# Gate stage with stationary tokens, three of eight pairs of k-tiles by seven block products, weight units of 1 MB, and part of h kept in DRAM

## The chip, the cores and the metric

The kernel runs on one core of one Trainium2 chip. The metric is the time of one execution on the device in microseconds (us), and the kernel before stands at the median of three runs. The engines are named as the profile names them: PE multiplies matrices (PEld is its loading of stationary operands), DVE, ACT and POOL work on vectors, SP issues most transfers.

## The reference

One layer of an encoder works on 256 tokens of width 2048, in float32: half a feed-forward step, a mixer (a long convolution beside differential attention), and a second half feed-forward step, each followed by a layer norm. The change is in the two feed-forward steps, whose inner width is 5632:

```python
def swiglu(x, w_gate, w_up, w_down):
    return (jax.nn.silu(x @ w_gate) * (x @ w_up)) @ w_down

x = layer_norm(ALPHA * x + 0.5 * swiglu(x, ffn1_w_gate[i], ffn1_w_up[i], ffn1_w_down[i]), ln1_g[i], ln1_b[i])
...
x = layer_norm(ALPHA * x + 0.5 * swiglu(x, ffn2_w_gate[i], ffn2_w_up[i], ffn2_w_down[i]), ln3_g[i], ln3_b[i])
```

The hidden rows are h = silu(x @ w_gate) * (x @ w_up), 256 x 5632.

## The kernel before, in words

**Precision.** Every float32 operand is cut into a high part (a cast on ACT) and a low part (a subtraction on DVE), and a product is the sum of three matmuls: high by high, high by low and low by high. `mm3` issues the three.

**Weights.** All weights pass once from DRAM, in pieces of 512 KB that the list `units` holds in the order of use. `fetch` issues their transfers on SP's queue into four raw slots, `prepare` cuts the next two pieces ahead of use (ACT at L176, DVE at L177) and `nextunit` hands the next piece to PE. `tick`, called once for each piece, moves the side work on (`beside`, `once`): generators that load vectors, compute the convolution's filter or finish an earlier block.

**Gate stage.** 22 blocks of 256 hidden columns. In `ws_block` the weights are stationary (128 x 128) and the tokens move: for each of the 16 k-tiles and each 128 columns, one matmul of 512 columns (the weights' high part by the tokens' high and low parts side by side, L395) and one of 256 (the low part by the tokens' high part, L396). A block's result lies transposed in PSUM, 256 tokens along the row. `gate` adds its two halves (`ws_sum`), applies silu, multiplies (POOL) and cuts h, which stays in SBUF as `hh` and `hl` for the whole down stage.

**Down stage.** Four chunks of 512 output columns. The h tiles are stationary, the weights move, 512 columns in each matmul (L94 to L96); a piece of 512 KB is two k-tiles, which is 12 matmuls. `scale_residual` loads and scales the rows of the residual `res`, and `last_vectors` the vectors of the last layer norm.

**Order of work.** Each engine runs its own instructions in order. A scheduler places them from the dependencies; `after` adds an order by hand, and the pools' buffer counts set what waits for what. The first feed-forward step has the tag 1, the last one 2 or 3. FFN1 and FFN2 below are those two steps.

Of the kernel before, what the change touches and what calls it, by code (L numbers as in the profile page):

```python
# [11 lines left out]
F32 = mybir.dt.float32  # L12
# [24 lines left out]
RAW = 4  # L37
READY = 2
AHEAD = 5
# [35 lines left out]
def kernel(ctx: ExitStack, tc: tile.TileContext, a: dict, out: bass.AP):  # L75
# [3 lines left out]
    wp = ctx.enter_context(tc.tile_pool(name="wp", bufs=4))  # L79
# [32 lines left out]

    units = []

    def ws_units(tag, w, c0, ws=None):

        for kq in range(KD // 4):
            for m, v in enumerate(ws or [w]):
                units.append((v[0][kq * 512:(kq + 1) * 512, c0:c0 + 256].rearrange("(k p) c -> p k c", p=P), 4, 256, f"{tag}_{kq}_{m}"))

    def as_units(tag, w, c0, kt):

        for ku in range(kt // 2):
            units.append((w[0][ku * 256:(ku + 1) * 256, c0:c0 + 512].rearrange("(k p) c -> p k c", p=P), 2, 512, f"{tag}_{ku}"))

    def ffn_units(tag, wg, wu, wd):
        for fb in range(FF // 256):
            ws_units(f"{tag}g{fb}", None, fb * 256, [wg, wu])
        for c in range(4):
            as_units(f"{tag}d{c}", wd, c * 512, KF)  # L130
# [8 lines left out]
    for k in range(KD):  # L139
        units.append((a["w_out"][0][k * P:(k + 1) * P, :1024].rearrange("p (k c) -> p k c", k=2), 2, 512, f"wo_{k}"))  # L140
# [4 lines left out]
    st = {"dma": 0, "split": 0, "use": 0}  # L145
    raws, parts = {}, {}
    hold = {}

    def halves(i, k):

        n = (4, 2)[i] if i < 2 else 1
        return [slice(q * k // n, (q + 1) * k // n) for q in range(n)]

    def fetch(n):
        while st["dma"] < min(n, len(units)):
            i = st["dma"]
            src, k, c, name = units[i]
            raws[i] = wp.tile([P, k, c], F32, tag="raw", name=f"raw{name}", bufs=RAW)
            for s_ in halves(i, k):
                nc.sync.dma_start(out=raws[i][:, s_], in_=src[:, s_])  # L160
            st["dma"] += 1

    def prepare(n):
        while st["split"] < min(n, len(units)):
            i = st["split"]
            _, k, c, name = units[i]
            late = i - (len(units) - LEAD)
            if 0 <= late < 4:

                hi, lo = (xx[:, 4 * late + 2 * q:4 * late + 2 * q + 2].rearrange("p k a l -> p k (a l)") for q in range(2))  # L170
            else:
                hi = wp.tile([P, k, c], F32R, tag="whi", name=f"hi{name}")
                lo = wp.tile([P, k, c], F32R, tag="wlo", name=f"lo{name}")
            raw = raws.pop(i)
            for s_ in halves(i, k):
                i1 = nc.scalar.copy(out=hi[:, s_], in_=raw[:, s_])  # L176
                i2 = nc.vector.tensor_tensor(out=lo[:, s_], in0=raw[:, s_], in1=hi[:, s_].bitcast(F32), op=ALU.subtract)  # L177
                if hold:
                    after(i1, hold["act"])
                    after(i2, hold["dve"])  # L180
                if i == 0 and s_.stop == 2:
                    xt_first(1, i1, i2)
            parts[i] = (hi, lo)
            st["split"] += 1
# [24 lines left out]
    def nextunit():  # L209
        i = st["use"]  # L210
        st["use"] += 1
        fetch(i + 1 + AHEAD)
        prepare(i + 1 + READY)
        tick()
        return parts.pop(i)
# [18 lines left out]
    for kp in range(KD // 2):  # L234
# [6 lines left out]
        if kp in (0, 1, 3):  # L241
            fetch({0: 1, 1: 2, 3: 4}[kp])
# [36 lines left out]

    def xt_first(kp, a1=None, a2=None):  # L280
# [12 lines left out]
    def xt_chunk(tag, c, g, b):  # L293
        for kp in (2 * c, 2 * c + 1):
# [17 lines left out]
            if kp == 1:  # L312
                hold["act"], hold["dve"] = i1, i2

# [120 lines left out]
    def ffn(tag, first, down_side=None, gate_side=None, filler=None, lead=2, between=None):  # L435
        with tc.tile_pool(name=f"ffn{tag}", bufs=1, reuse_waits="tile") as fp:
            hh = fp.tile([P, KF, L], F32R, name=f"hh{tag}")
            hl = fp.tile([P, KF, L], F32R, name=f"hl{tag}")

            def gate(f, pg, pu):  # L440
                sg = sm.tile([P, L], F32, tag="sg", name=f"sg{tag}_{f}")
                ws_sum(sg, pg)
                nc.scalar.activation(out=sg, in_=sg, func=AF.Silu)
                hf = sm.tile([P, L], F32, tag="hf", name=f"hf{tag}_{f}")
                ws_sum(hf, pu)
                nc.gpsimd.tensor_tensor(out=hf, in0=hf, in1=sg, op=ALU.mult)  # L446
                split(hh[:, f, :], hl[:, f, :], hf, nc.gpsimd)

            first(0)
            for fb in range(FF // 256):  # L450
                if fb == 12 and gate_side is not None:
                    beside(gate_side)
                ps = [[bank(f"ps{tag}_{fb}_{m}_{t}") for t in range(2)] for m in range(2)]
                for kq in range(4):
                    for m in range(2):
# [688 lines left out]
```

## Time and profile before

| what | value |
|---|---|
| median of 3 runs | 1941.37 us (1941.0 to 1942.09) |
| profiled execution | 1940.2 us, its span 1938.4 us |
| PE busy | 1921.0 us (99%) |
| DVE busy | 1214.8 us (63%) |
| ACT busy | 926.5 us (48%) |
| POOL busy | 298.3 us (15%) |
| granted TensorE clock, mean | 0.998 |
| read from DRAM | 366.28 MB |

The span runs from the first instruction to the last; the profiled execution's own time is 1.8 us longer. Busy shares are averages over the whole span: an engine at 63% can still be late in one place. PE's busy time is the sum of modelled ends, so its pace is read from the starts of its matmuls.

### The profile page before, as it was taken

Reading aid. Unit: us, or ns where it says so; the run is one execution under the profiler, and the core shown is the slowest. Engines: PE = TensorE matmul, PEld = TensorE weight load, DVE = VectorE, ACT = ScalarE, POOL = GpSimd, SP = SyncE. Lnnn points to the kernel's source line nnn. Section 1 sums busy time; section 2 is a strip of 40 time slices with the busy share of each in tenths; the row PEclk is TensorE's granted clock in tenths of the full one; section 3 lists DMA queues with packets and bytes.
Section 4 is the critical chain, followed back from the end, with each engine's and each line's share of the span. In section 5 each row is a group of like instructions: output and inputs, shape, how many; then the busy total and the mean of one; then the engine's idle time right before and its main releaser. Section 6 shows DMA issues by size and latency. Waiting matters only on the chain. (4 is left out here: it accounts for less than half of the span.)

```text
span 1938.4 us, 27298 instructions
## 1 busy us (share of the span) xinstructions
PE 1921.0 (99%) x10360; PEld 1650.8 (85%) x10360; DVE 1214.8 (63%) x1555; ACT 926.5 (48%) x1336; POOL 298.3 (15%) x327
## 2 busy tenths in 40 slices
PE   9999999999999999999999999999999999999999
PEld 7888888888888888888888888888888888888887
DVE  6555556555566656899978766755555555544555
ACT  5454444455444445555555544545444445433332
POOL 4221111112100001112222011311211112100000
PEclk9999999999999999999999999999999999999999
DMA  8665656665666656755575445856566665565553
GB/s 286 211 192 185 195 188 199 186 193 186 206 207 226 211 193 204 236 176 163 176 218 164 161 155 162 278 188 192 188 192 189 190 190 185 193 195 192 193 193 131
DMA packets 295028, 376.47 MB, mean 194 GB/s; under 512 B 13331, under 2 KB 222892, under 8 KB 294896
## 3 DMA queue, kind: packets, MB, share of 16 engines
q1 hardware_dynamic: 289728, 361.38, 58.0%
q0 software_dynamic: 4736, 12.82, 2.2%
q8 instruction: 81, 1.33, 0.3%
q10 hardware_dynamic: 432, 0.52, 0.1%
q14 instruction: 51, 0.42, 0.1%
HBM read 366.28 MB, written 8.39 MB: 193 GB/s over the span
## 5 line engine op out<-in xcount | busy, mean ns | idle before, releaser
L395 PE MATMUL ps<-xx,hi1g 128*128 128x512 f32 x1408 | 489.3, 392 | 1.7 <-DVE xx L99 1.3
L395 PE MATMUL ps<-xx,hi2g 128*128 128x512 f32 x1408 | 488.7, 394 | 1.1 <-DVE xx L99 1.1
L396 PE MATMUL ps<-xx,lo1g 128*128 128x256 f32 x1408 | 393.6, 280 | 1.0 <-DVE lo1g L177 1.0
L396 PE MATMUL ps<-xx,lo2g 128*128 128x256 f32 x1408 | 390.0, 277 | 0.0
L177 DVE TENSOR_TENSOR lo2g<-raw2g,hi2g 128x1024 fp32r<-128x1024 f32 x176 | 235.0, 1337 | 178.4 <-ACT hi2g L176 178.4
L177 DVE TENSOR_TENSOR lo1g<-raw1g,hi1g 128x1024 fp32r<-128x1024 f32 (+1 forms) x180 | 230.8, 1285 | 178.6 <-ACT hi1g L176 178.3
L395 PEld LDWEIGHTS ps<-xx,hi2g 128*128 128x128 f32 x1408 | 263.9, 188 | 62.4 <-ACT xt L305 1.3
L395 PEld LDWEIGHTS ps<-xx,hi1g 128*128 128x128 f32 x1408 | 263.2, 187 | 61.0 <-ACT hi1g L176 2.3
L176 ACT CAST hi2g<-raw2g 128x1024 fp32r<-128x1024 f32 x176 | 185.2, 1053 | 187.1 <-PE ps L395 176.3
L176 ACT CAST hi1g<-raw1g 128x1024 fp32r<-128x1024 f32 (+1 forms) x180 | 185.7, 1035 | 175.2 <-PE ps L395 165.9
L396 PEld LDWEIGHTS ps<-xx,lo1g 128*128 128x128 f32 x1408 | 265.8, 189 | 2.1 <-DVE lo1g L177 1.9
L396 PEld LDWEIGHTS ps<-xx,lo2g 128*128 128x128 f32 x1408 | 264.2, 188 | 0.1
L446 POOL TENSOR_TENSOR hf<-hf,sg 128x256 f32<-128x256 f32 x88 | 66.1, 770 | 738.8 <-DVE hf L400 738.7
L177 DVE TENSOR_TENSOR lo2d<-raw2d,hi2d 128x1024 fp32r<-128x1024 f32 x84 | 103.5, 1233 | 109.2 <-ACT hi2d L176 109.0
L176 ACT CAST hi1d<-raw1d 128x1024 fp32r<-128x1024 f32 x88 | 92.7, 1053 | 125.0 <-PE pd L96 114.8
L176 ACT CAST hi2d<-raw2d 128x1024 fp32r<-128x1024 f32 x84 | 88.6, 1055 | 130.1 <-PE pd L96 123.9
L177 DVE TENSOR_TENSOR lo1d<-raw1d,hi1d 128x1024 fp32r<-128x1024 f32 x88 | 107.1, 1222 | 67.4 <-ACT hi1d L176 67.4
L395 PE MATMUL ph<-xx,hihy 128*128 128x512 f32 x384 | 137.9, 402 | 2.2 <-DVE xx L99 1.1
L95 PE MATMUL pd<-lo1d,hh 128*128 128x512 f32 (+1 forms) x356 | 137.8, 387 | 0.0
L94 PE MATMUL pd<-hi1d,hh 128*128 128x512 f32 (+1 forms) x356 | 137.8, 387 | 0.0
L96 PE MATMUL pd<-hi1d,hl 128*128 128x512 f32 (+1 forms) x356 | 137.7, 387 | 0.0
L94 PE MATMUL pd<-hi2d,hh 128*128 128x512 f32 (+1 forms) x344 | 132.1, 384 | 0.0
(387 smaller groups left out, 3090.1 us busy)
## 6 DMA issues: line engine op xcount, KB each, us to landing
raw1d<-in_ffn_w_down_dram SPq DMA_DIRECT2D x88, 512.0 KB, 4.3
raw2g<-in_ffn_w_gate_dram SPq DMA_DIRECT2D x88, 512.0 KB, 3.4
raw2g<-in_ffn_w_up_dram SPq DMA_DIRECT2D x88, 512.0 KB, 3.4
raw2d<-in_ffn_w_down_dram SPq DMA_DIRECT2D x88, 512.0 KB, 4.3
raw1g<-in_ffn_w_gate_dram SPq DMA_DIRECT2D x87, 512.0 KB, 3.5
raw1g<-in_ffn_w_up_dram SPq DMA_DIRECT2D x87, 512.0 KB, 3.8
rawhy<-in_w_in_dram SPq DMA_DIRECT2D x48, 512.0 KB, 4.3
rawat<-in_w_in_dram SPq DMA_DIRECT2D x48, 512.0 KB, 4.2
```

The source lines that it names most:

```text
L94: mm(out=o, lhsT=lh, rhs=rh, start=start, stop=False)
L95: mm(out=o, lhsT=lh, rhs=rl, start=False, stop=False)
L96: mm(out=o, lhsT=ll, rhs=rh, start=False, stop=stop)
L176: i1 = nc.scalar.copy(out=hi[:, s_], in_=raw[:, s_])
L177: i2 = nc.vector.tensor_tensor(out=lo[:, s_], in0=raw[:, s_], in1=hi[:, s_].bitcast(F32), op=ALU.subtract)
L395: mm(out=ps[t], lhsT=h[:, k, ts_], rhs=xx[:, kk].rearrange("p a l -> p (a l)"), start=kk == 0, stop=False)
L396: mm(out=ps[t][:, :L], lhsT=lo[:, k, ts_], rhs=xx[:, kk, 0, :], start=False, stop=kk == KD - 1)
L446: nc.gpsimd.tensor_tensor(out=hf, in0=hf, in1=sg, op=ALU.mult)
```

## The change

The gate stage is turned round and its loop is rebuilt:

- **Tokens are stationary and weights move**, as in the down stage. There are 11 blocks of 512 hidden columns. A product of one k-tile of tokens for one half of the tokens with 512 columns of one matrix is three matmuls of 512 columns (`mm3`). A pair of k-tiles needs eight such products (two k-tiles, two halves of the tokens, w_up and w_gate).
- **Seven instead of eight.** In the blocks after the first, three of the eight pairs (`NS = 3`) go by a seven-product scheme of the Strassen kind for 2 x 2 blocks. Its sums of tokens are made once for each feed-forward step (`sums_of`); its sums of weights, t1 to t4, are made anew for each such pair on DVE (L245 to L247), with a high part on ACT (L248) and a low part on DVE (L250). The block's results are put together on DVE (L621 to L625, and `finish`).
- **Units of 1 MB.** One unit holds both matrices of a pair of k-tiles. Kind S is a pair of seven products, kind N one of eight, and H two pieces of 512 KB as before. There are two raw slots and two slots of high and low parts, and in the gate stage a third of each (`res[:, 0]` as the raw one; `res[:, 1]` holds t1 to t4).
- **Turning h.** The block's rows of h now lie with the tokens on the partitions. `turn` makes h-transposed by four transposes on PE for each 256 columns (L556). For the first 26 of the 44 k-tiles of h the result is copied by ACT (L561) and written to DRAM from ACT's queue (L562); the last 18 (`NR = 18`) are cut and stay in SBUF (`h2`).
- **Reading h back.** In the down stage `back` reads the 26 tiles on SP's queue, 128 KB each (L659), through four small tiles, and cuts them into `h1`. Each chunk of the down stage begins with the 18 tiles that stayed.
- **Moved.** `res` being in use, the rows of the residual are loaded in the down stage (in FFN2 from a copy that POOL's queue has written to DRAM, `xn2`), `filter_net` goes from FFN1's gate stage to its down stage, and `last_vectors` goes behind `scale_residual`.

The core of the diff:

```diff
-RAW = 4
-READY = 2
-AHEAD = 5
+NS = 3
+NR = 18
+NP = KD // 2
+NF = FF // 512
...
+    def gate_order(fb):
+        if fb == 0:
+            return [(kp, False) for kp in range(NP)]
+        return [(0, True), (3, False), (1, True), (4, False), (2, True), (5, False), (6, False), (7, False)]
...
+                th, tl = (gate[q][:, st["t"] % 2] for q in ("th", "tl"))
+                st["t"] += 1
+                t = res[:, 1, :].rearrange("p (k c) -> p k c", c=512)
+                nc.scalar.copy(out=hi[:, 1:4], in_=raw[:, 1:4])
+                nc.vector.tensor_tensor(out=t[:, 0:2], in0=raw[:, 0:1].to_broadcast([P, 2, 512]), in1=raw[:, 1:3], op=ALU.subtract)
+                nc.vector.tensor_tensor(out=t[:, 2], in0=raw[:, 1], in1=t[:, 1], op=ALU.subtract)
+                nc.vector.tensor_tensor(out=t[:, 3], in0=raw[:, 3], in1=t[:, 2], op=ALU.subtract)
+                nc.scalar.copy(out=th, in_=t)
+                sub(nc.vector, lo[:, 1:4], raw[:, 1:4], hi[:, 1:4])
+                sub(nc.vector, tl, t, th)
...
-                        ws_block(ps[m], *nextunit(), kq, (lambda: first(kq + 1)) if more else None)
...
+            def turn(fb, rows, q):
+                pt = bank(f"pt{tag}_{fb}_{q}")
+                for f in range(2):
+                    for j in range(2):
+                        c = (2 * q + f) * P
+                        nc.tensor.transpose(out=pt[:, f * L + j * P:f * L + (j + 1) * P], in_=rows[j][:, c:c + P], identity=ident)
+                pv = pt.rearrange("p (f l) -> p f l", l=L)
+                k = fb * 4 + 2 * q
+                if k < n1:
+                    t = t512(f"turn{tag}_{k}")
+                    nc.scalar.copy(out=t, in_=pv)
+                    nc.scalar.dma_start(out=h1d[:, k:k + 2, :], in_=t)
+                else:
+                    k -= n1
+                    split(h2[:, 0, k:k + 2, :], h2[:, 1, k:k + 2, :], pv)
...
+                def finish(j, i):
+                    ps = pc["abcd"[2 * j + i]]
+                    if n_seven:
+                        o = (rows, up)[i][j]
+                        nc.vector.tensor_tensor(out=o, in0=ps, in1=o, op=ALU.add)
+                        ps = o
+                    if i == 0:
+                        nc.scalar.activation(out=rows[j], in_=ps, func=AF.Silu)
+                    else:
+                        nc.vector.tensor_tensor(out=rows[j], in0=ps, in1=rows[j], op=ALU.mult)
...
+                    if seven:
+                        t3, t1, t2, t4 = ((th[:, q], tl[:, q]) for q in range(4))
+                        s_last = all(not s_ for _, s_ in order[n + 1:])
+                        todo = {
+                            "1": (x_of(k1, 0), g1, s_last), "a": (x_of(k2, 0), g2, False),
+                            "b": (sum_of(kp, 2), u2, False), "7": (sum_of(kp, 3), t3, s_last),
+                            "5": (sum_of(kp, 0), t1, s_last), "6": (sum_of(kp, 1), t2, s_last),
+                            "c": (x_of(k2, 1), t4, False),
+                        }
+                        for key in ("1756abc" if n == 0 else "1ab756c"):
+                            add(key, *todo[key])
+                        turn_next()
+                        tick()
+                        if s_last:
+                            nc.scalar.copy(out=rows[0], in_=pp["1"])
+                            nc.vector.tensor_tensor(out=up[0], in0=pp["6"], in1=rows[0], op=ALU.add)
+                            nc.vector.tensor_tensor(out=rows[1], in0=pp["7"], in1=up[0], op=ALU.add)
+                            nc.vector.tensor_tensor(out=up[0], in0=pp["5"], in1=up[0], op=ALU.add)
+                            nc.vector.tensor_tensor(out=up[1], in0=pp["5"], in1=rows[1], op=ALU.add)
+                        continue
+                    for i, w in enumerate(((g1, g2), (u1, u2))):
+                        for ks in ([(0,), (1,)] if fb == 0 and not last_ else [(0, 1)]):
+                            for j in range(2):
+                                for k in ks:
+                                    add("abcd"[2 * j + i], x_of((k1, k2)[k], j), w[k], last_ and k == 1)
+                                if last_:
+                                    finish(j, i)
...
+                        if i == 0:
+                            turn_next()
+                            tick()
...
+            def back():
+                turn_next()
+                yield 1
+                turn_next()
+                yield 1
+                for k in range(n1):
+                    t = sm.tile([P, L], F32, tag="sg" if k % 2 == 0 else "hf", name=f"back{tag}_{k}")
+                    nc.sync.dma_start(out=t, in_=h1d[:, k, :])
+                    split(h1[:, 0, k, :], h1[:, 1, k, :], t)
+                    if k % 3 == 2:
+                        yield 1
```

**Where instructions stand, ACT.** The piece is the start of the seventh block of FFN1, of what ACT does before the turns of the sixth block. In the names, `hi_ring` and `hi_125` are the slots of high parts, `th` the high parts of t1 to t4, `row` the block's hidden rows, `pt` the bank of a turn. First the kernel before, at a block's end:

```order
L399 COPY sg_4_782<-ps_2_0_0_566 128x256 [waits PE_49]
L176 CAST hi1g_1_0_778<-raw1g_1_0_702 128x1024 [waits DMAHW0_49,DVE_49,PE_49]
L443 ACTIVATE sg_4_782<-sg_4_782 128x256 [waits DVE_49]
L399 COPY sg_5_792<-ps_2_0_1_567 128x256 [waits PE_49]
L399 COPY hf_4_786<-ps_2_1_0_568 128x256 [waits PE_49,Pool_49]
L443 ACTIVATE sg_5_792<-sg_5_792 128x256 [waits DVE_49]
L399 COPY hf_5_796<-ps_2_1_1_569 128x256 [waits PE_49,Pool_49]
L176 CAST hi1g_1_1_820<-raw1g_1_1_726 128x1024 [waits DMAHW1_49,Activation_49]
```

There the copies of 256 columns out of PSUM stand between casts of 1024. After the change:

```order
L198 CAST hi_ring<-raw_ring 128x2048 [waits DMAHW1_49,DMAHW2_49,PE_49,Activation_49]
L599 ACTIVATE row_5_0_1556<-row_5_0_1556 128x512 [waits DVE_49]
L599 ACTIVATE row_5_1_1557<-row_5_1_1557 128x512 [waits DVE_49]
L243 CAST hi_ring<-raw_ring 128x1536 [waits DMAHW3_49,DMAHW4_49,PE_49,Activation_49]
L198 CAST hi_125<-res 128x2048 [waits DMAHW5_49,DMAHW6_49,PE_49,Activation_49]
L248 CAST th_123<-res 128x2048 [waits DVE_49]
L561 COPY turn_20_1873<-pt_5_0_1868 128x512 [waits PE_49]
L562 DMA h1d_118<-turn_20_1873 128x512 [waits Activation_49]
L561 COPY turn_22_1897<-pt_5_1_1892 128x512 [waits PE_49]
```

The copy of `pt_5_0` now stands behind one cast of 1536 columns and two of 2048, the last of which waits for DVE's t1 to t4.

**PE.** The same place on PE: the second turn of the sixth block inside the second unit of the seventh. `pb`, `pd` and `pt` are banks of PSUM. Before, at the change from one pair of banks to the next:

```order
L396 MATMUL ps_9_0_0_1976<-xx,lo1g_1_0_1983 128x256
L395 MATMUL ps_9_0_1_1977<-xx,hi1g_1_0_1982 128x512
L396 MATMUL ps_9_0_1_1977<-xx,lo1g_1_0_1983 128x256
L395 MATMUL ps_9_1_0_1978<-xx,hi1g_1_1_2024 128x512 [waits Activation_49]
L396 MATMUL ps_9_1_0_1978<-xx,lo1g_1_1_2025 128x256 [waits DVE_49]
```

There a bank is taken over from ACT at L395, between pairs of 512 and 256 columns. After the change:

```order
L95 MATMUL pb_6_1860<-hi_ring,xx 128x512
L96 MATMUL pb_6_1860<-lo_ring,xx 128x512
L556 MATMUL pt_5_1_1892<-ident,row_5_0_1556 128x128 [waits Activation_49]
L556 MATMUL pt_5_1_1892<-ident,row_5_1_1557 128x128
L556 MATMUL pt_5_1_1892<-ident,row_5_0_1556 128x128
L556 MATMUL pt_5_1_1892<-ident,row_5_1_1557 128x128
L97 MATMUL pb_6_1860<-hi_ring,xx 128x512
L95 MATMUL pb_6_1860<-hi_ring,xx 128x512
L96 MATMUL pb_6_1860<-lo_ring,xx 128x512
L97 MATMUL pb_6_1860<-hi_ring,xx 128x512
L95 MATMUL pd_6_1906<-hi_ring,xx 128x512 [waits Activation_49]
```

The four transposes into `pt_5_1` wait for ACT, and behind them on PE's queue the first product into `pd_6` waits for ACT again.

**SP.** The start of FFN1's down stage on SP's queue: transfers of down weights, and those of h. Before:

```order
L160 DMA raw1d_0_4521<-in_ffn_w_down_dram 128x2x512 [waits DMAHW6_49,DVE_49]
L160 DMA raw1d_1_4543<-in_ffn_w_down_dram 128x2x512 [waits DMAHW7_49,DVE_49]
L160 DMA raw1d_2_4565<-in_ffn_w_down_dram 128x2x512 [waits DMAHW0_49,DVE_49]
L160 DMA raw1d_3_4587<-in_ffn_w_down_dram 128x2x512 [waits DMAHW1_49,DVE_49]
L160 DMA raw1d_4_4609<-in_ffn_w_down_dram 128x2x512 [waits DMAHW2_49,DVE_49]
```

There pieces of weights alone follow each other. After the change:

```order
L194 DMA raw_ring<-in_ffn_w_down_dram 128x2x512 [waits DVE_49]
L659 DMA back_0_3249<-h1d_118 128x256 [waits DMAHW3_49]
L659 DMA back_1_3253<-h1d_118 128x256 [waits DMASW6_49,DMASW5_49,DMASW7_49,DMASW4_49,DMAHW4_49,DMASW1_49,DMASW0_49]
L659 DMA back_3_3277<-h1d_118 128x256 [waits DMASW3_49,DMAHW5_49,DMASW2_49,DVE_49]
L659 DMA back_2_3257<-h1d_118 128x256 [waits DMAHW6_49,DMAHW3_49,DVE_49]
L659 DMA back_4_3281<-h1d_118 128x256 [waits DMAHW7_49,Activation_49]
L194 DMA raw_ring<-in_ffn_w_down_dram 128x2x512 [waits DMAHW0_49,DVE_49]
L659 DMA back_5_3285<-h1d_118 128x256 [waits DMAHW4_49,DMAHW1_49,DVE_49]
L659 DMA back_7_3311<-h1d_118 128x256 [waits DMAHW5_49,DMAHW2_49,DVE_49]
L194 DMA raw_ring<-in_ffn_w_down_dram 128x2x512 [waits DVE_49]
L659 DMA back_6_3307<-h1d_118 128x256 [waits DMAHW6_49,DVE_49]
```

Two or more read-backs now stand between two pieces of weights, most of them waiting for DVE's cut of an earlier read-back.

## Rows read from the trace of the kernel before

**Rows 1.** The page: busy time, share and instructions of each engine; granted clock by slice.

```profile
PE 1921.0 (99%) x10360; PEld 1650.8 (85%) x10360; DVE 1214.8 (63%) x1555; ACT 926.5 (48%) x1336; POOL 298.3 (15%) x327
...
PEclk9999999999999999999999999999999999999999
```

**Rows 2.** Windows: us, busy (instructions) of PE, PEld, DVE, ACT, POOL, clock, DMA, GB/s.

```profile
10.00:15.00 5.00, 4.51 (x27) 3.63 (x26) 3.61 (x4) 3.66 (x6) 2.28 (x5) 1.00 0.98 345
...
1240.00:1680.00 440.00, 440.00 (x2540) 384.63 (x2539) 242.08 (x239) 215.91 (x320) 77.41 (x80) 1.00 0.61 193
1720.00:1840.00 120.00, 120.00 (x531) 99.36 (x530) 59.22 (x54) 46.42 (x44) 0.00 (x0) 1.00 0.59 194
```

**Rows 3.** The page's groups: FFN1's and FFN2's wide gate matmuls.

```profile
L395 PE MATMUL ps<-xx,hi1g 128*128 128x512 f32 x1408 | 489.3, 392 | 1.7 <-DVE xx L99 1.3
L395 PE MATMUL ps<-xx,hi2g 128*128 128x512 f32 x1408 | 488.7, 394 | 1.1 <-DVE xx L99 1.1
```

**Rows 4.** Timeline of PE, gate stage: start, us, instruction.

```profile
99.86 0.39 PE L395 MATMUL ps<-xx,hi1g 128*128 128x512 f32 x1
100.09 0.28 PE L396 MATMUL ps<-xx,lo1g 128*128 128x256 f32 x1
...
103.67 0.39 PE L395 MATMUL ps<-xx,hi1g 128*128 128x512 f32 x1
```

**Rows 5.** Timeline of PE, down stage.

```profile
1768.61 0.39 PE L94 MATMUL pd<-hi2d,hh 128*128 128x512 f32 x1
...
1772.69 0.39 PE L94 MATMUL pd<-hi2d,hh 128*128 128x512 f32 x1
```

**Rows 6.** Chain that ended last, 1204 to 1213: start, us, piece.

```profile
1204.91 0.87 PE ps_xt L301 x8
1205.78 0.23 PE ps L395
```

**Rows 7.** Instructions of L301, the transposes: min/median/max in ns.

```profile
L301 PE MATMUL ps_xt<-ident,res x64: 270/272/328, 759.1 to 1211.9; 128*128 128x128 f32 x64
```

**Rows 8.** Timeline of DVE, 1220 to 1225.

```profile
1219.74 0.68 DVE L339 SCALAR_TENSOR_TENSOR res<-b,res 128x512 f32<-128x512 f32 x1
1220.35 0.41 DVE L400 TENSOR_TENSOR sg<-ps,sg 128x256 f32<-128x256 f32 x1
1220.68 0.68 DVE L337 SCALAR_TENSOR_TENSOR res<-res,g 128x512 f32<-128x512 f32 x1
1221.28 1.22 DVE L177 TENSOR_TENSOR lo2g<-raw2g,hi2g 128x1024 fp32r<-128x1024 f32 x1
1222.41 0.68 DVE L339 SCALAR_TENSOR_TENSOR res<-b,res 128x512 f32<-128x512 f32 x1
```

**Rows 9.** Timeline of ACT, 42 to 46.

```profile
42.65 2.00 ACT L176 CAST hi1g<-raw1g 128x1024 fp32r<-128x1024 f32 x2
```

**Rows 10.** Groups of ACT: busy, mean ns; idle before, what ended it.

```profile
L176 ACT CAST hi1g<-raw1g 128x1024 fp32r<-128x1024 f32 (+1 forms) x180 | 185.7, 1035 | 175.2 <-PE ps L395 165.9 <-DMA raw1g<-in_ffn_w_gate_dram 2.7 <-PE ps L396 2.0
...
L399 ACT COPY sg<-ps 128x256 f32<-128x256 f32 x88 | 32.5, 369 | 64.7 <-PE ps L396 64.7
...
L102 ACT CAST wh<-pw 128x512 fp32r<-128x512 f32 x8 | 4.7, 593 | 1.3 <-PE pw L970 1.3
```

**Rows 11.** Transfers: queue, count, KB each, median us to landing.

```profile
raw2g<-in_ffn_w_up_dram SPq DMA_DIRECT2D x88, 512.0 KB, 3.4
...
raw2d<-in_ffn_w_down_dram SPq DMA_DIRECT2D x88, 512.0 KB, 4.3
...
res<-in_x_dram SPq DMA_DIRECT2D x4, 512.0 KB, 6.0
fr<-in_filt_w_out_dram SPq DMA_DIRECT2D x16, 128.0 KB, 4.9
...
c_fwd_raw<-in_c_fwd_dram SPq DMA_DIRECT2D x2, 256.0 KB, 8.7
```

**Rows 12.** Waits of PE: for what, us in total, times, longest.

```profile
PE ps L395 <- DVE xx L99: 2.4, 2, 1.3
```

More of the change, by code (lines that the diff above doesn't have):

```diff
@@ L143 @@
     ffn_units("2", a["ffn2_w_gate"], a["ffn2_w_up"], a["ffn2_w_down"])
-    st = {"dma": 0, "split": 0, "use": 0}
+    st = {"dma": 0, "split": 0, "use": 0, "t": 0, "cut": 0, "unit": 0}
     raws, parts = {}, {}
     hold = {}
-    def halves(i, k):
-        n = (4, 2)[i] if i < 2 else 1
-        return [slice(q * k // n, (q + 1) * k // n) for q in range(n)]
+    raw_ring = wp.tile([P, 2, 2048], F32, name="raw_ring")
+    hi_ring = wp.tile([P, 2, 2048], F32R, name="hi_ring")
+    lo_ring = wp.tile([P, 2, 2048], F32R, name="lo_ring")
@@ L154, in fetch, with turn_over @@
+    raw_at = [raw_ring[:, i] for i in range(2)]
+    cut_at = [(hi_ring[:, i], lo_ring[:, i]) for i in range(2)]
+    gate = {}
+    def turn_over(places):
+        places.append(places.pop(0))
+        return places[-1]
     def fetch(n):
-        while st["dma"] < min(n, len(units)):
+        n = steps[min(n, len(steps)) - 1][0] + 1
+        while st["dma"] < n:
             i = st["dma"]
[L157 to L160, printed above, removed]
-            st["dma"] += 1
@@ L163, in prepare @@
-    def prepare(n):
[L164 to L170, printed above, removed]
-            else:
[L172 to L184, printed above, removed]
+            kind, name, src = units[i]
@@ new lines, in fetch @@
+            if kind == "H" and len(raw_at) > 2:
+                raw_at[:] = [v for v in raw_at if v is not gate["raw"]]
+            if i - st["cut"] >= len(raw_at):
+                return
+            st["dma"] += 1
+            raws[i] = turn_over(raw_at)
+            for m in ((0, 1) if kind == "H" else (1, 0)):
+                k = src[m].shape[1]
+                o = raws[i][:, m * 1024:(m + 1) * 1024].rearrange("p (k c) -> p k c", k=k)
+                for s_ in ([slice(q, q + 1) for q in range(k)] if i < 2 else [slice(0, k)]):
+                    nc.sync.dma_start(out=o[:, s_], in_=src[m][:, s_])
@@ L313, in xt_chunk @@
                 hold["act"], hold["dve"] = i1, i2
+            if sv is not None and kp < NS:
+                later.append((sv, kp, t))
+            turned["dve"] = hold["dve"] if kp in (3, 5, 7) else i2
+    later = []
     def warm(n):
@@ L432, in as_last @@
         return pd
-    def ffn(tag, first, down_side=None, gate_side=None, filler=None, lead=2, between=None):
-        with tc.tile_pool(name=f"ffn{tag}", bufs=1, reuse_waits="tile") as fp:
[L437 to L455, printed above, removed]
-                        more = fb == 0 and kq < 3 and m == 0
-                        ws_block(ps[m], *nextunit(), kq, (lambda: first(kq + 1)) if more else None)
-                for t in range(2):
-                    once(gate, fb * 2 + t, ps[0][t], ps[1][t])
-            if down_side is not None:
-                beside(down_side)
@@ L467, in ffn @@
+            beside(back())
             for c in range(4):
@@ L1037, with first2, down2 @@
     ln2 = ln
-    def first2(c):
+    xn2 = dr.tile([P, 2, D], F32, name="xn2")
+    def first2(c, sv):
         if c == 0:
             normalise(ln2, 0)
-        xt_chunk("2", c, 2, 3)
+        xt_chunk("2", c, 2, 3, sv)
         if c < 3:
             normalise(ln2, c + 1)
-        if c == 3:
-            beside(scale_residual("2", "ln2_g", "ln2_b"))
+        while later and c > 0:
+            once(sums_of, *later.pop(0))
+        cs = slice(c * 512, (c + 1) * 512)
+        nc.gpsimd.dma_start(out=xn2[:, :, cs], in_=res[:, :, cs])
+    def down2():
+        for c in range(4):
+            cs = slice(c * 512, (c + 1) * 512)
+            nc.sync.dma_start(out=res[:, :, cs], in_=xn2[:, :, cs])
+        yield 2
+        yield from scale_residual("2", "ln2_g", "ln2_b")
+        yield from last_vectors()
     gb3 = {}
```

185 lines of the change are left out of this document (153 added, 32 removed).

## The prediction

> **What bounds the kernel now.** First the page's busy line [rows 1]: PE works 1921.0 of 1938.4 us, and its granted clock is full in every slice. Then the waits [rows 12]: the longest sum for one cause is 2.4 us. So the time is PE's queue of matmuls at its own pace, and the change pays by what it takes off that queue, if nothing makes PE wait instead. Pace is read from starts, since the ends are modelled: 392 ns for a 512-column matmul [rows 3] would give more work than there is time. In the gate stage, starts from 99.86 to 103.67 are 11 pairs of a 512- and a 256-column matmul [rows 4]: 3.81 / 11 = 0.3464 us. The window of 440 us holds 2540 matmuls, 1270 pairs: 0.3465 [rows 2]. In the down stage, 18 matmuls of 512 columns start from 1768.61 to 1772.69 [rows 5]: 0.2267 us each. DVE is busy 242 of 440 us in the gate stage, ACT 216 [rows 2]: room, if late work is not in one place.
>
> **The change part by part.** *Matmuls.* Before, two gate stages of 1408 pairs [rows 3]: 2816 x 0.3464 = 975.5 us. After, a pair of k-tiles needs 8 products x 3 = 24 matmuls, or 21 by seven products. A first block is 192, each other 5 x 24 + 3 x 21 = 183; two steps of 192 + 10 x 183 are 4044. The form, h or tokens stationary and 512 columns of weights moving, is that of the down stage, so 4044 x 0.2267 = 916.8 us. That is **-58.7**. About two thirds are not the seven products: with eight everywhere the count is 4224, 957.6 us, already 17.9 less than before; the seven products take 40.8 more.
>
> *Turns.* 2 x 11 x 2 turns of four transposes, 176. Eight of the same shape take 0.87 us of PE's path [rows 6], 0.109 each: **+19.1**. Their duration is 272 ns [rows 7]; were none overlapped it would be 47.9.
>
> *The wait at the second turn.* Seven banks collect a seven-product block, and the first turn takes the eighth. So the second turn waits for ACT's copy of the first, and the product `pd` behind it for the copy of the second; all else on PE stands behind them. When does ACT copy? Its queue has a cast of 1536 columns, one of 2048, and th of 2048 ahead of the copy, and th waits for t1 to t4 on DVE. Durations: DVE starts lie 0.61 or 0.60 us apart after 512 columns, 0.33 after 256, 1.13 after 1024 [rows 8]; the line through them gives 1.67 for 1536 and 2.20 for 2048 (an estimate). An operation that needs the one before it pays about 0.1 more (my allowance). On ACT two casts of 1024 take 2.00 together [rows 9] and one 1.04 by itself [rows 10], so they start 0.95 apart; 256 more columns cost 0.22 in copies [rows 10], so I put 2048 at 0.95 + 0.85 = 1.80 (estimate). The copy of 512 out of PSUM is 0.59 [rows 10].
>
> Let a seven-product block start at 0. A unit of 21 matmuls is 4.76 us, one of 24 is 5.44, a turn 0.44. The last three units of the block before start at -16.3, -10.9 and -5.4. The last unit's high part can be cut when the first of these has freed its slot, so from -16.1 to -14.2, and DVE goes on from there without a gap: the low part of it (-12.0), three sums of 512 with the first unit's t1, t2 among them (-9.1), t3, t4 (-7.7), two low parts (th being ready at -5.8; -3.5), t1 and t2 of the third unit (-2.4), the finish of the block before with the second unit's low part between (3.5), and t3, a low part and t4 of the third unit (6.4). The rows of h are done at 3.5; the first turn wants them at 4.76. ACT's cast of 2048 waits for the first unit's end and ends at 6.76; th then takes until 8.56 and the copy until 9.15. PE reaches the second turn after a turn and 14 matmuls: 5.20 + 14 x 0.2267 = 8.37. It waits **0.8 us**, in each of 20 blocks: **+16**. Bounds: 0, were the casts each a few tenths shorter (B), and 2.2 a block, 44, were DVE 1.7 later (C). I take 0.8, the starts as they stand in the rows. In the blocks whose turns stay in SBUF the copy is a cast and the subtraction beside it, and the order differs a little; I take the same.
>
> *DVE and ACT as a whole.* DVE has 36 us of work in a seven-product block (18.6 in three S units of 1.13 + 0.60 + 0.60 + 1.67 + 2.20, 11 in five N units, 6 in ten sums and finishes), against 183 x 0.2267 and the turns and waits, 43: not the bound, but nearly. POOL, which made low parts and products before [rows 1], falls out of the gate stage.
>
> *Transfers.* The bytes of weights are the same and moved at 193 GB/s [rows 2]. A unit of 1 MB lands in some 4.9 us (3.4 for 512 KB [rows 11], and 1.5 more at 345 GB/s [rows 2], an estimate), and there are three slots, each unit lasting 4.8 to 5.4: hidden. The transfers of h to DRAM are issued on ACT's queue behind the copies that PE waits for (half a us each, my allowance); only the second copy stands behind one, and its bank is ready no sooner.
>
> *Down stage.* Each chunk starts with the 18 tiles in SBUF: 9 pieces of 12 matmuls, 2.72 us each, 24.5 us. In the next 13 pieces, 35.4 us, the first chunk needs the 26 tiles read back. Weights, tiles and the residual are 6.8 + 3.4 + 2.1 = 12.3 MB; less a lead of four pieces, 288 GB/s, under the 345 that a window reached [rows 2]. The tiles share SP's queue with the weights. A tile's time is 4.9 us to land [rows 11] and about 0.4 each for a cast and a subtraction of 256 columns [rows 8, 10], with perhaps 0.8 (my allowance) in two queues: 6.5 over four small tiles, 1.63 each. Two to a piece are 3.27 against 2.72: over 13 pieces the weights fall 7.1 us behind, which a lead of four pieces, 10.9, covers. **+3** for both steps (0 to 40, see D).
>
> *Cost nothing:* the loads of the residual, `filter_net` and the last vectors, moved beside a down stage in which DVE is busy 59 of 120 us and ACT 46 [rows 2]; without that cover, a few us. The start of FFN1 with 1 MB units: +0.5 (-2 to +3). The mixer keeps its forms.
>
> *Sum:* -58.7 + 19.1 + 16 + 3 + 0.5 = -20.1, against the profiled execution's 1940.2 (span and 1.8 around it): 1920.1. The median stands 1.2 above that execution: **1921**.
>
> **The rivals.** *B, the wait is hidden.* If casts of 2048 take 0.3 less than my line, the copy meets PE: -36, about **1904**. For it: no row shows 2048. Against: it needs ACT and DVE both quicker.
>
> *C, DVE is later.* If an operation holds DVE for its duration, 0.68 and 1.22 [rows 8], and not the 0.60 and 1.13 between starts, 20 of them from the last low part to t4 cost 20 x 0.085 = 1.7 more. 0.4 of that is slack before th; 1.3 lands on the turn: 2.1 a block, +26 in all, **1947**, slower. The gain is gone from 1.0 us more a block. Against it: the starts in the rows do overlap, though those are short operations. The Trainium skill (VectorE: DVE Perf Modes, "The TRN2 errata") gives (N + 151) / 0.96 ns for an fp32 tensor_tensor, 691 at 512 and 2291 at 2048, as a fixed cost that each instruction pays. By that 2048 would take 0.09 more than my line, and the sum would be that of C; the rows agree with its 691 as a duration, and disagree as a distance between starts.
>
> *D, SP's queue is held by the tiles.* The lead is used up from 1.78 us a tile ((10.9 / 13 + 2.72) / 2), and each us above costs 26 in each step. Were landing as slow as the 8.7 of one row [rows 11], a tile is 2.58 and 21 us are lost in each step: about **1960**, slower; the gain is gone from 2.17 a tile, a landing of 7. For it: the queue is in order and weights stand behind tiles. Against: 4.9 was measured for the same size and queue.
>
> *E, transposes of full duration*, 272 ns [rows 7]: +28.7, **1950**. Against it: eight in 0.87 us [rows 6]. The Trainium skill (TensorE: Matmul & The Clock Gate, "Part 4: PE-mode transpose") has about 275 ns for one inside a kernel; that agrees with the duration here, but not with the path's 0.109.
>
> **How the numbers follow.** The forecast, 1905 to 1936 by itself, 0.58; B 0.12; C 0.11; D 0.10; E 0.04; something not seen 0.05. The range 1899 to 1948 holds the forecast, B and most of C, and leaves out most of D, E and the unseen. 0.2% is 3.9 us, about what a measurement here can tell from no change. Faster than 1937.5: forecast, B, a little of C and of the unseen, 0.76; within, the milder C and D, 0.07; slower 0.17.
>
> **What would show it.** Gate matmuls 0.2267 apart; in all turns a wait of PE at L556 for ACT's copy at L561, 0.5 to 1.5 us each in 20 blocks, and little else; gate stages of 476 us each ((916.8 + 19.1 + 16) / 2) against 488 for the pairs before; a first chunk of the down stage without waits for weights. Wrong if PE waits at each unit for low parts of DVE, if the waits at L556 are above 2 us (C) or absent (B), if the first chunk of a down stage is over 5 us longer than the second (D), or if a turn takes over 0.8 us (E).

## The result and the profile after

The changed kernel takes 1916.0 us (median; 1915.1 to 1918.7) against 1941.2 before: a ratio of 0.987 (0.986 to 0.989), 25 us faster. The prediction was 1921, in a range of 1899 to 1948. The profiled execution has a span of 1914.5 us, 23.9 less than before.

The page of the changed kernel, its busy line and its DRAM traffic; these answer to [rows 1]:

```profile
PE 1889.5 (99%) x8948; PEld 1567.2 (82%) x8948; DVE 1490.0 (78%) x1759; ACT 948.3 (50%) x1046; POOL 136.9 (7%) x155
...
HBM read 375.20 MB, written 17.30 MB: 205 GB/s over the span
```

PE still works 99% of the time, with 1412 fewer instructions. DVE has gone from 63% to 78%, and POOL is left with 137 us of its 298. The read-back of h and the copies of the residual add 9 MB each way.

By windows, as in [rows 2], the first line is inside FFN2's gate stage, the second inside its down stage (the columns are those of that group):

```profile
1240.00:1640.00 400.00, 399.65 (x1790) 327.95 (x1791) 345.27 (x286) 206.96 (x151) 2.20 (x4) 1.00 0.62 210
1720.00:1840.00 120.00, 120.00 (x531) 99.37 (x530) 59.40 (x54) 46.42 (x44) 0.00 (x0) 1.00 0.56 194
```

DVE is busy 345 of 400 us in the gate stage, 86%; before, it was 242 of 440. The down stage is as it was.

The start of a block on PE, FFN1's fourth (start, us, instruction; it answers to [rows 4 to 6]):

```profile
140.00 0.39 PE L95 MATMUL p<-hi,xx 128*128 128x512 f32 x1
...
144.54 0.39 PE L97 MATMUL pc<-th,xx 128*128 128x512 f32 x1
144.77 0.60 PE L556 MATMUL pt<-ident,row 128*128 128x128 f32 x4
145.12 0.48 PE L95 MATMUL pa<-hi_ring,xx 128*128 128x512 f32 x1
145.44 0.40 PE L96 MATMUL pa<-lo_ring,xx 128*128 128x512 f32 x1
...
148.20 0.39 PE L96 MATMUL pb<-lo_ring,xx 128*128 128x512 f32 x1
148.58 0.66 PE L556 MATMUL pt<-ident,row 128*128 128x128 f32 x4
148.99 0.47 PE L97 MATMUL pb<-hi_ring,xx 128*128 128x512 f32 x1
```

From 140.00 to 144.54 are 20 matmuls: 0.227 us each. A turn shows 0.35 to the next matmul and leaves that one 0.09 late: 0.44. The second turn starts 0.38 after the matmul before it, where 0.23 would be no wait: 0.15, and the matmul behind it starts another 0.06 late: 0.2 in all.

What ACT does meanwhile:

```profile
144.33 1.91 ACT L198 CAST hi<-res 128x2048 fp32r<-128x2048 f32 x1 [2.60 <-PE pb L97]
146.14 1.90 ACT L248 CAST th<-res 128x2048 fp32r<-128x2048 f32 x1
147.95 0.58 ACT L561 COPY turn<-pt 128x512 f32<-128x512 f32 x1
```

The cast of 2048 waits for PE's product `pb`, not for the unit's end (the product `pc` from th follows on PE); cast, th and copy then follow 1.81 us apart, and the copy's end (147.95 + 0.58 = 148.53) lets the second turn go. On DVE, ahead of the same block, an operation of 2048 lasts 2.28, and the next one starts 2.20 after it:

```profile
123.88 2.28 DVE L100 TENSOR_TENSOR lo_ring<-raw_ring,hi_ring 128x2048 fp32r<-128x2048 f32 x1
126.08 0.68 DVE L623 TENSOR_TENSOR row<-p,up 128x512 f32<-128x512 f32 x1
```

The waits of PE, as in [rows 12] (for what, us, times, longest):

```profile
PE pa L96 <- DVE lo_ring L100: 2.4, 2, 1.8
PE pt L556 <- DVE row L601: 2.1, 1, 2.1
PE pf L815 <- ACT xx L103: 2.0, 1, 2.0
...
PE pt L556 <- ACT turn L561: 1.8, 2, 0.9
```

The first is the start of FFN1. The second is the first turn of FFN2's last block: its place is the start of the down stage, and its rows are not yet done. The third is the filter in FFN1's down stage. The last are the second turns in the first block with seven products of each step, where ACT's casts before the copy had to wait for weights.

### The profile page after: what moved, and what is told of

The parts are those of the page before. It is cut to its first block, busy times and chain, and to the rows that moved or that the text cites. A ratio compares the mean times of both kernels' runs of the same rounds, so it can differ in the third digit from the quotient of the medians.

```text
span 1914.5 us, 23807 instructions
## 1 busy us (share of the span) xinstructions
PE 1889.5 (99%) x8948; PEld 1567.2 (82%) x8948; DVE 1490.0 (78%) x1759; ACT 948.3 (50%) x1046; POOL 136.9 (7%) x155
## 5 line engine op out<-in xcount | busy, mean ns | idle before, releaser
L100 DVE TENSOR_TENSOR lo_ring<-raw_ring,hi_ring 128x1024 fp32r<-128x1024 f32 (+2 forms) x396 | 562.6, 1423 | 260.1 <-ACT hi_ring L198 253.8
L198 ACT CAST hi_ring<-raw_ring 128x1024 fp32r<-128x1024 f32 (+1 forms) x366 | 432.9, 1184 | 468.0 <-PE pd L97 255.9
L95 PE MATMUL pd<-hi_ring,h 128*128 128x512 f32 (+1 forms) x700 | 271.5, 388 | 0.0
L96 PE MATMUL pd<-lo_ring,h 128*128 128x512 f32 (+1 forms) x700 | 271.0, 387 | 0.1
L97 PE MATMUL pd<-hi_ring,h 128*128 128x512 f32 (+1 forms) x700 | 270.8, 387 | 0.0
L95 PEld LDWEIGHTS pd<-hi_ring,h 128*128 128x128 f32 x700 | 132.3, 189 | 26.9 <-issue 0.7
L97 PEld LDWEIGHTS pd<-hi_ring,h 128*128 128x128 f32 x700 | 132.1, 189 | 26.7
L96 PEld LDWEIGHTS pd<-lo_ring,h 128*128 128x128 f32 x700 | 132.0, 189 | 26.0 <-DVE lo_ring L100 0.5
L100 DVE TENSOR_TENSOR tl<-res,th 128x2048 fp32r<-128x2048 f32 x60 | 137.3, 2288 | 7.3 <-ACT th L248 6.4
L471 PE MATMUL ph<-xx,hi_ring 128*128 128x512 f32 x384 | 136.9, 400 | 2.2 <-DVE xx L100 1.1
L248 ACT CAST th<-res 128x2048 fp32r<-128x2048 f32 x60 | 114.6, 1910 | 13.0 <-DVE res L247 13.0
L95 PE MATMUL pa<-hi_ring,xx 128*128 128x512 f32 x194 | 77.0, 397 | 0.5 <-DVE xx L378 0.5
L97 PE MATMUL pa<-hi_ring,xx 128*128 128x512 f32 x194 | 75.8, 390 | 0.0
L95 PE MATMUL p<-th,sums 128*128 128x512 f32 x180 | 70.2, 390 | 0.0
L97 PE MATMUL p<-th,sums 128*128 128x512 f32 x180 | 70.1, 389 | 0.0
```

Source lines behind the costliest of these rows:

```text
L95: mm(out=o, lhsT=lh, rhs=rh, start=start, stop=False)
L96: mm(out=o, lhsT=lh, rhs=rl, start=False, stop=False)
L97: mm(out=o, lhsT=ll, rhs=rh, start=False, stop=stop)
L100: return eng.tensor_tensor(out=o, in0=x, in1=h.bitcast(F32), op=ALU.subtract)
L198: i1 = nc.scalar.copy(out=hi, in_=raw)
L248: nc.scalar.copy(out=th, in_=t)
```

## The experiments

Each run is compared with the kernel before, timed beside it. Where two changed kernels are compared, the difference of their ratios (times 1941 us) stands beside that of their medians. The length of a gate stage is read from the trace, from its first matmul to the first of the down stage; that of a down stage from its first matmul to its last.

**No seven products.** All pairs by eight, all else as changed:

```diff
-        return [(0, True), (3, False), (1, True), (4, False), (2, True), (5, False), (6, False), (7, False)]
+        return [(kp, False) for kp in (0, 3, 1, 4, 2, 5, 6, 7)]
```

> All pairs of k-tiles by eight products, all else as in the changed kernel. Theory (PE's queue of matmuls sets the time): 180 more matmuls in each feed-forward step, 2 x 180 x 0.2267 = 40.8 us more, 0.9 to 1.06 us a block less of waits at the second turn in the two first blocks and about 0.2 in the others, 4 to 5 in all, since only four banks collect: 1916 + 41 - 5 = 1952, slower than the kernel before. Rival (the gain comes from moving weights of 512 columns and units of 1 MB, and what the seven products save is paid back by their sums on DVE): 1916 to 1930.

Measured 1947.8 us, ratio to the kernel before 1.0018 (1.0007 to 1.0029). That is 28 (by the ratios) to 32 us (by the medians) more than with seven products, against 36 expected. Turning the stage, larger units and DRAM for h do not pay by themselves: the 17.9 us by which the new form is quicker go into the turns' 19.1. The two gate stages take 984.6 us together here, 986.0 before the change and 951.9 in the changed kernel.

**Two pairs of seven products.**

```diff
-        return [(0, True), (3, False), (1, True), (4, False), (2, True), (5, False), (6, False), (7, False)]
+        return [(0, True), (3, False), (1, True), (4, False), (2, False), (5, False), (6, False), (7, False)]
```

> Two pairs of eight by seven products in place of three (the last of the three is done by eight). Theory: 3 x 10 x 2 = 60 more matmuls, 13.6 us: 1929.6; the waits at the turns stay, as the first three units of a block do. Rival (DVE's load sets part of the pace, so that a lighter block gains back): 1916 to 1924.

Measured 1929.0, ratio 0.993 (0.991 to 0.995): 11 (by the ratios) to 13 us (by the medians) for a pair, for 13.6 by the count. The expectation that the waits at the turns stay was wrong. DVE is now done with t4 before the block starts, th is cast before it too, and the copy follows the cast of 2048 at once (the fourth block):

```profile
145.38 1.91 ACT L198 CAST hi<-res 128x2048 fp32r<-128x2048 f32 x1 [2.60 <-PE pb L97]
147.19 0.57 ACT L561 COPY turn<-pt 128x512 f32<-128x512 f32 x1
```

In 12 blocks the second turn starts 0.23 after the matmul before it, without a wait, and such a block is 0.43 us longer than with three pairs (43.13 for 42.70), not 3 x 0.2267 = 0.68. So a lighter DVE does give back 0.25 us in each of these blocks, 3 in all and less than the rival had. Other waits have grown: the two gate stages together are 12.4 us longer than with three pairs.

**Four pairs.**

```diff
-NS = 3
-NR = 18
+NS = 4
+NR = 16
...
+        return [(0, True), (4, False), (1, True), (5, False), (2, True), (6, False), (3, True), (7, False)]
```

> Four pairs of eight by seven products, S and N units in turn; two more of the 44 tiles of h go through DRAM, for the room in SBUF (NR = 16). Theory by count alone: 13.6 us less, 1902.5. But DVE's work in a block rises from 36 to 40 us against 180 x 0.2267 + 0.9 = 41.7, so I expect waits of PE for DVE and ACT of up to 0.7 us a block, 1903 to 1917. Rival C in its sharper form (DVE becomes the bound): above 1920.

Measured 1962.6, ratio 1.010 (1.007 to 1.013): 44 (by the ratios) to 47 us (by the medians) slower than with three, far from my expectation. A window in FFN2's gate stage, then among the waits of PE's loading of operands, and of PE itself:

```profile
1240.00:1640.00 400.00, 385.72 (x1690) 310.25 (x1689) 355.92 (x300) 211.92 (x155) 1.60 (x1) 0.99 0.59 200
```

```profile
PEld p L95 <- ACT th L248: 31.6, 36, 2.3
PEld p L95 <- ACT hi_ring L243: 12.2, 11, 1.4
...
PE p L95 <- ACT th L248: 18.0, 14, 2.0
```

The loading now waits for th of the S units themselves, 36 times, and PE stands for it 14 times. DVE is busy 356 of 400 us, 89%, so it is not full. I take it that the chain from weights over t1 to t4 and th to PE is too long for units that follow so closely; no run tests that or tells which link to shorten, and the part that two more tiles through DRAM have in the loss was not taken apart.

**The slot free sooner.** In a block's first unit the products with high parts come earlier:

```diff
-                        for key in ("1756abc" if n == 0 else "1ab756c"):
+                        for key in ("1a7b56c" if n == 0 else "1ab756c"):
```

> The first unit of a block does its three products with high parts of weights earlier, so that the slot that ACT waits for is free some 1.4 us sooner (2.7 us after the block's start in place of 4.1). Theory (the second turn waits for the chain slot, cast of 2048, th, copy on ACT): the waits at the second turn go to zero in the blocks where they are 0.2, and stay in the two first blocks, which wait for weights: 2.5 to 4 us less, 1912 to 1913.5. Rival (the 0.2 is PE's own cost of changing to transposes, or the banks): 1916.

Measured 1912.2 (1910.4 to 1917.8), ratio to the kernel before 0.984 (0.982 to 0.987). The interval overlaps that of the changed kernel, so the total does not settle it; the trace shows whether the wait is gone. ACT's chain in the fourth block (which starts at 141.29 here) ends before PE wants the second turn:

```profile
144.25 1.92 ACT L198 CAST hi<-res 128x2048 fp32r<-128x2048 f32 x1 [1.24 <-PE pb L97]
146.29 1.92 ACT L248 CAST th<-res 128x2048 fp32r<-128x2048 f32 x1
148.10 0.59 ACT L561 COPY turn<-pt 128x512 f32<-128x512 f32 x1
```

In 12 blocks the second turn starts 0.23 after the matmul before it, and a block's period falls from 42.70 to 42.45 us: the wait there is gone, by way of the slot. The total agrees with the expectation by luck. The 3 us that these 12 blocks save are lost again in the same stages (a second turn that starts 1.06 after the matmul before it in FFN1's tenth block, one that starts 2.38 after it in FFN2's first with seven products, where it was 1.30, and a stretch at a granted clock of 0.50 at the start of FFN1): the gate stages take 952.0 us for 951.9. The 3.7 us by which this trace's span is shorter lie in the down stages, above all at FFN1's filter, which the edit does not touch.

**The slot free later.** The same unit with the products of high parts last, and the second turn held at its place by an order among PE's instructions:

```diff
-                        for key in ("1756abc" if n == 0 else "1ab756c"):
+                        for key in ("756c1ab" if n == 0 else "1ab756c"):
...
+                                        tr = turn(*turns.pop(0), behind=m2)
```

> The first unit of a block does its three products with high parts of weights last, so that their slot is free at the unit's end, 4.76 us after the block's start, as the prediction had it, and not at 4.08; the second turn is held at its place behind 14 matmuls of the second unit. Theory (slot, cast, th, copy, second turn is one chain): each second turn waits 0.7 us longer, 0.85 in place of 0.15, in 14 to 20 blocks: 10 to 14 us more, 1926 to 1930. Rival (the wait is no chain from the slot): 1916 to 1918.

Measured 1960.6, ratio 1.010 (1.008 to 1.011), far over. In the blocks whose turns go to DRAM the second turn starts 1.06 after the matmul before it, as the theory has it. But held in its place it starts 3.9 after the matmul before it in the six blocks whose turns stay in SBUF, where it waits for a subtraction in DVE's queue (21.1 us in six waits), and behind these waits the clock falls (below). So it was run again with the edit in 12 blocks alone, the second to the seventh of each step:

```diff
+                held = fb > 0 and fb * 4 - 2 < n1
...
-                        for key in ("1756abc" if n == 0 else "1ab756c"):
+                        for key in (("756c1ab" if held else "1756abc") if n == 0 else "1ab756c"):
```

> As the kernel whose slot is free late, but only in the 12 blocks whose second turn waits for the copy of a first turn that goes to DRAM; the other blocks are those of the changed kernel. In the late run before, the trace had 1.06 us before the second turn in these blocks in place of 0.38, and 3.9 us in six blocks whose turns stay in SBUF. Theory: 12 x 0.68 = 8 us more, 1924, and no stretch at the lower clock in the gate stages. Rival (waits of under 1 us also take the clock down, so each costs more than its length): above 1930.

Measured 1923.9, ratio 0.991 (0.989 to 0.992): 7.9 us more by the medians, 6.6 by the ratios, for an expected 8. The 12 blocks are not quite those that the expectation meant: ten of them waited for the slot, two are the first with seven products, which wait for weights, and the eighth block of each step, which waited for the slot too, is left as it was. The ten now take 43.37 us for 42.70, 6.7 us of the 7.4 by which the gate stages are longer. ACT and PE in the fourth block, which starts at 141.38:

```profile
146.39 1.91 ACT L199 CAST hi<-res 128x2048 fp32r<-128x2048 f32 x1 [3.28 <-PE pb L97]
148.20 1.91 ACT L249 CAST th<-res 128x2048 fp32r<-128x2048 f32 x1
150.01 0.57 ACT L564 COPY turn<-pt 128x512 f32<-128x512 f32 x1
```

```profile
149.58 0.39 PE L643 MATMUL pb<-lo_ring,xx 128*128 128x512 f32 x1
150.63 0.66 PE L557 MATMUL pt<-ident,row 128*128 128x128 f32 x4 [0.67 <-ACT turn L564]
```

The cast starts 5.0 after the block, the copy ends at 9.2, and the turn starts 1.05 after the matmul before it: a wait of 0.82. That is the prediction's walk to a tenth of a us, for the order of products that the prediction took: copy's end 9.15, wait 0.8.

**th twice.** One more cast ahead of the copy, the second turn held as above:

```diff
-                nc.scalar.copy(out=th, in_=t)
+                for _ in range(1 + name.endswith("_1")):
+                    gate["th_cast"] = nc.scalar.copy(out=th, in_=t)
...
+                    if fb > 0:
+                        after(i1, gate["th_cast"])
...
```

> ACT casts the high part of t1 to t4 of a block's third unit twice, ahead of the copy of the first turn (1.81 us more); the second turn is held at its place. Theory: the copy is 1.8 us later in each of 20 blocks and PE waits for it: 28 to 36 us more, 1944 to 1952, and the gain against the kernel before is gone; this is the price that rival C had for a late copy. Rival (ACT has room, it is busy half the time): 1916 to 1920.

Measured 1960.4, ratio 1.009 (1.008 to 1.011), more than expected. The waits that the expectation spoke of are there, and others that holding the turn brings:

```profile
PE pt L558 <- ACT turn L565: 25.7, 14, 2.2
PE pt L558 <- DVE h L101: 10.1, 6, 3.6
```

14 waits of 1.84 for ACT. In 12 of these blocks the second turn starts 2.31 or more after the matmul before it, where it was 0.38: with the turn held, a copy 1.8 us later costs PE 1.9. The 10.1 are the six blocks whose turns stay in SBUF; the rest is not taken apart.

**Each transpose twice.**

```diff
-                for f in range(2):
+                for f in (0, 1, 0, 1):
```

> Every turn does its four transposes twice into the same bank. Theory (a transpose costs PE's path 0.109 us): 176 x 0.109 = 19.2 more, less the waits of 0.2 that the longer first turn covers, 3: 1932 to 1935. Rival E (a transpose costs its duration of 0.272): 1916 + 47.9 = 1964.

Measured 1938.2, ratio 0.998 (0.997 to 0.999). The fourth block's first turn:

```profile
148.53 1.03 PE L556 MATMUL pt<-ident,row 128*128 128x128 f32 x8
149.32 0.48 PE L95 MATMUL pa<-hi_ring,xx 128*128 128x512 f32 x1
```

Eight take 0.79 where four took 0.35: 0.11 each. The longer first turn does not cover the waits of 0.2: the second turn still starts 0.4 after the matmul before it in the same 12 blocks. Beyond 1935, the wait at the end of FFN2's gate stage is 5.0 us here for 2.1. Rival E, a transpose of full duration, is out.

**Two tiles for the read-back.**

```diff
-                    t = sm.tile([P, L], F32, tag="sg" if k % 2 == 0 else "hf", name=f"back{tag}_{k}")
+                    t = sm.tile([P, L], F32, tag="sg", name=f"back{tag}_{k}")
```

> The tiles of h are read back through two small tiles in place of four. Theory D as the prediction has it (SP's queue is held by the read-backs): a tile's time doubles to some 3.2 us, over the 1.78 at which the weights' lead is used up, 26 x 1.4 = 37 us in each step: up to 1990; the trace shows read-backs starting 3 us (FFN1) and 13 us (FFN2) ahead of the down stage, so rather 1950 to 1985. Rival (only the lateness of the last tile counts, weights pass by): 81 us of reading against 60 to 70 until they are needed, 10 us a step, 1930 to 1940.

Measured 1941.4, ratio 0.9995 (0.998 to 1.001): 24 (by the ratios) to 25 us (by the medians) more than with four tiles. The waits of PE:

```profile
PE pd L95 <- ACT h L103: 14.0, 8, 3.4
PE pt L556 <- DVE row L601: 5.5, 1, 5.5
```

PE waits for the tiles of h themselves, 7 of the 8 times in FFN1's down stage, and in neither down stage does it wait for weights. FFN1's 26 tiles are issued 3.05 us apart here, where they were 1.79 apart with four small tiles. By D, 26 x (3.05 - 1.78) = 33 us would be lost at weights; FFN1's down stage is 18.6 us longer, at tiles, and FFN2's 1.3. So SP's queue is not what D said: the weights get past, and it is the late tile that costs. The 5.5 is the end of FFN2's gate stage, 2.1 in the changed kernel; why it differs between runs is not shown.

**Three edits together.**

```diff
-                        for key in ("1756abc" if n == 0 else "1ab756c"):
+                        for key in ("1a7b56c" if n == 0 else "1ab756c"):
...
+            def late_turns():
+                yield 2
+                turn_next()
+                yield 1
+                turn_next()
...
-        yield 3
+        yield 5
         ft()
```

> Three edits together: the early slot; the two last turns of a gate stage two pieces later in the down stage, where their rows are done; and two pieces more between the loads of the filter's table and its use. Theory: 3.5 for the slot as measured alone, 2.2 and 2.0 us of waits at the start of FFN2's down stage and in FFN1's, and with each the stretch at half the clock behind it (1.6 us each by the trace): 1916 - 3.5 - 7.4 = 1905 to 1909. Rival (the clock's stretches come whatever PE waits for, or the waits move elsewhere): 1910 to 1913.

Measured 1913.6 (1911.5 to 1914.5), ratio 0.986 (0.984 to 0.987): no gain over the early slot alone, and by the intervals none over the changed kernel either. The two waits aimed at are gone, and others stand in their place:

```profile
PE pt L556 <- ACT turn L561: 3.6, 2, 2.4
PE ps_f L753 <- ACT fh L748: 2.0, 1, 2.0
...
PE pd L95 <- ACT hi_ring L198: 1.7, 1, 1.7
```

They are the first block with seven products in FFN2, an earlier step of the filter, and the weights in FFN2's down stage.

## Why the prediction was right

*Matmuls, -58.7.* Right: the pace of the down stage holds in the gate stage (0.227). With none and with two pairs of seven products the gate stages are 32.7 and 12.4 us longer, for 40.8 and 13.6 by the count. With none, 7.3 us of waits have gone, which is most of the difference; with two, 2.4 have gone and others grown. One sentence there is the wrong way round: of 58.7, the form gives 17.9 and the seven products 40.8, so two thirds are the seven products.

*Turns, +19.1.* Right: 0.44 a turn, and doubling the transposes adds 0.11 for each.

*The wait at the second turn, +16.* The place and the mechanism were right, the size was not: the extra time at the second turns adds up to 5.0 (0.2 in 12 blocks, 1.1 in two, nearly nothing in six). The step that failed is "ACT's cast of 2048 waits for the first unit's end and ends at 6.76". In the trace of the changed kernel it waits for `pb`, the third product from the weights' high parts, and starts 4.33 after the block: the unit's last product takes t4, which lies in th, and needs the slot no more. The order of the seven keys, with t4's product last, stands in the diff. With the order as the prediction took it, the wait was 0.82. Estimates that the walk needed held: 1.81 between ACT's casts of 2048 for 1.80, 2.20 on DVE for 2.20, and in the run with that order 9.2 for the copy's end for 9.15. It erred elsewhere too, without effect: DVE started its chain some 2 us sooner than in the walk (the low part at 123.88 is 16.1 before the block, for 14.2) and so was not late in this block, t4 being done at 5.0 for 6.4. And the two first blocks wait for weights, which it had not seen.

*Down stages and start, +3 and +0.5.* The first was mis-sized, by a wait that I had costed at nothing. Summed over PE's starts, what goes beyond its pace has grown by 5.6 us in FFN1's and by 2.2 in FFN2's, and none of it at a wait of PE for tiles read back. In FFN1's it is for the most part the moved filter, whose tables come late behind weights and tiles, and the lower clock behind that wait; in FFN2's for the most part the lower clock behind the wait with which the gate stage ends. The first chunk is 3.5 and 3.0 us longer than the second, under the 5 that the prediction set as D's sign. FFN1 starts 1.4 later, for 0.5.

*The end of FFN2's gate stage* was not in the sum: 2.3 us until the last block's rows are done.

Together: the term of the turns' wait was 11.0 too high; the end of FFN2's gate stage (2.3 for nothing), the down stages (7.8 for 3) and the start (1.4 for 0.5) were 8.0 too low. From -20.1 that makes -23.1, against -23.9 in the spans; the mixer is some 1 us shorter. That the sum came nearer than its terms is luck. So is the sign "gate stages of 476 us each": they last 475.7 and 476.2, but of some 17 us in them beyond matmuls and turns the second turns have 5.0, and the rest is elsewhere, 3.3 at FFN1's start, 2.3 at the end of FFN2's stage, 2.6 in transposes of x in FFN2 among it. The sign that named the wait itself, 0.5 to 1.5 us in 20 blocks, did not come.

*The rivals.* B was nearly what happened at the second turn, by another cause than it gave (the slot, not shorter casts). C did not happen: operations of 2048 on DVE follow each other 2.20 apart, though each lasts 2288 ns in the mean of 60. The Trainium skill's figure of 2291 ns (VectorE: DVE Perf Modes, "The TRN2 errata") agrees with that duration here, not with the distance between two. C's price for a late copy is right all the same, where the turn is held in its place: a copy 1.8 us later made 14 waits of 1.84. D did not happen, and its mechanism did not show with tiles 3.05 us apart either. E is out.

## What to carry to other kernels

Find which instruction frees a slot: not the last one of the unit that uses it, but the last one that reads that buffer, and the order inside a unit moves it without one matmul more. Then look where the saved time went: here the wait went away, and others of the same size came in its place. Where an engine is full, count its instructions by their distance between starts; that gave 13.6 us for a pair of seven products, and 11 to 13 were measured for the third, until at the fourth the time rose by some 45. A form that costs as much as it saves (here the turned stage) can still be worth it for what it makes possible.

## What the runs showed of the hardware

PE's clock falls behind some of PE's waits, and each such wait costs more than its length. In the run with the late slot, PE stood from 368.4 to 371.9 (windows of 2 us; the column ahead of the last two is the granted clock):

```profile
368.00:370.00 2.00, 0.41 (x2) 0.00 (x0) 2.00 (x2) 1.03 (x2) 0.00 (x0) 1.00 0.31 118
370.00:372.00 2.00, 0.08 (x1) 0.08 (x2) 2.00 (x3) 0.00 (x0) 0.00 (x0) 0.75 0.88 218
372.00:374.00 2.00, 2.00 (x7) 1.81 (x8) 1.97 (x3) 0.59 (x1) 0.00 (x0) 0.50 0.79 306
374.00:376.00 2.00, 2.00 (x6) 1.29 (x6) 0.98 (x2) 0.93 (x1) 0.00 (x0) 0.50 0.00 0
376.00:378.00 2.00, 2.00 (x7) 1.57 (x6) 1.00 (x1) 1.52 (x2) 0.00 (x0) 0.54 0.00 0
378.00:380.00 2.00, 2.00 (x11) 1.64 (x10) 2.00 (x2) 1.15 (x2) 0.00 (x0) 1.00 0.04 8
```

At 0.50, the level of 1.2 GHz, matmuls of 512 columns start 0.43 us apart, at 1.00, 2.4 GHz, 0.227: the wait of 3.5 is followed by some 3 us more. The changed kernel has this behind its wait of 2.0 for the filter (the eight matmuls from 532 to 534 are for the most part of 256 columns):

```profile
528.00:530.00 2.00, 0.42 (x2) 0.00 (x0) 1.28 (x4) 2.00 (x4) 0.00 (x0) 1.00 0.76 204
530.00:532.00 2.00, 1.19 (x5) 0.77 (x6) 1.71 (x2) 1.33 (x2) 0.00 (x0) 0.86 0.83 301
532.00:534.00 2.00, 2.00 (x8) 1.88 (x9) 1.19 (x2) 0.00 (x0) 0.00 (x0) 0.50 0.79 266
534.00:536.00 2.00, 2.00 (x8) 1.59 (x7) 1.27 (x2) 0.00 (x0) 0.55 (x1) 0.79 0.79 263
```

In the run with the slot late in 12 blocks, with waits of 0.7 us at most at the turns to DRAM, the granted clock is 1.00 from 60 to 480 and from 1240 to 1655, where these turns stand.
